# Split weights in half-tile buffers: six of 1024 columns in place of three of 2048

## The chip, the cores and the metric

The kernel runs on one core of one Trainium2 chip. The metric is the device time of one execution in microseconds; the number to predict is the median of the runs of the changed kernel.

## The reference

A trunk of two layers on one sequence of 256 tokens, width 1024, all in float32. Layer 0 mixes tokens by a mixture of three dilated sliding-window attentions, layer 1 by a gated linear attention (GLA); behind each stands a gated ConvFFN of inner width 2816. Each sub-layer is normed, and shifted, scaled and gated by a conditioning vector c.

```python
for i in range(DEPTH):                                   # DEPTH = 2
    mod = jax.nn.silu(c) @ w_ada[i] + b_ada[i]
    sh1, sc1, g1, sh2, sc2, g2 = jnp.split(mod, 6, axis=-1)
    h = rmsnorm(x, norm_mix[i]) * (1.0 + sc1) + sh1
    y = dilated_mixture(h, ...) if i % 2 == 0 else gla_mixer(h, ...)
    x = x + g1 * y
    h = rmsnorm(x, norm_ffn[i]) * (1.0 + sc2) + sh2
    x = x + g2 * conv_ffn(h, w_up[i], conv_w[i], conv_b[i], w_down[i])
return rmsnorm(x, norm_final)

def dilated_mixture(h, w_in, w_out, rel_bias):
    qkv = (h @ w_in).reshape(B, S, 3, 3, 16, 64)         # 3 groups, q k v, 16 heads
    outs, lses = zip(*[dilated_branch(...) for window, dilation in ((128, 1), (512, 4), (2048, 16))])
    o = jnp.sum(jax.nn.softmax(jnp.stack(lses), axis=0)[..., None] * jnp.stack(outs), axis=0)
    return o.reshape(B, S, 1024) @ w_out

def conv_ffn(h, w_up, conv_w, conv_b, w_down):
    u = conv_b + sum(conv_w[j] * shifted(h @ w_up, j) for j in range(3))
    a, b = jnp.split(u, 2, axis=-1)
    return (jax.nn.silu(a) * b) @ w_down
```

## The kernel before

Activations lie transposed, 128 channels of the width by 256 tokens in a tile, so that a width of 1024 is eight slices, kt = 0 to 7. Nearly all matrix products are made by `mm3` (lines 171 to 177) in three matmuls: each operand is split into a high part (rounded to the format fp32r) and a low part (the rest), and high times high (L175), low times high (L176) and high times low (L177) are summed in PSUM. Of the normed activations the parts are `hhi` and `hlo`, made by `normed` (L253): VectorE (DVE) writes `xr` (L257), ScalarE (ACT) `hhi` (L259), DVE `hlo` (L260). Of the weights they are `whi` and `wlo`, made by `split`: SyncE (SP) issues the load into `raw` (L159), ACT casts it to `whi` in two halves (L165), DVE subtracts to get `wlo` in two halves (L169). A tile of raw weights has up to 2048 columns. There are four buffers of `raw`, three of `whi` and three of `wlo`. A buffer is free for the next tile when the last product that reads it is done; so a cast to `whi` waits for matmuls. `parts` picks the columns of one product out of a split tile. Some other tiles share the buffers of `whi` and `wlo`: the conditioning row and the one-hot table of the bias at the start, the squares of x, and the output y at the end.

The order of the work is the scheduler's. The kernel is written down in program order, the tile framework schedules it with a timeline of its own, and pools, waits and `behind(...)` (an instruction isn't issued before the named ones) shape what comes out. Each engine then takes its instructions strictly in the order of the program so made, and each transfer is issued in the order of SP's queue.

The stages, in order of time:

- The start and the first pass. Loads of x, c and small tables, the first norm; then, for each kt, a tile of adaLN weights (`ada_chunk`: DVE makes two dot products at L138, ACT two `mod` columns at L148 and L146), `normed`, and `split` of the tile `w0[kt]` of 15 x 128 columns: six blocks of q and k of head pair 0, three of v, six of q and k of head pair 1. Eight PSUM banks sum the products over kt: `pqk` (q and k of pair 0), `pv`, `pqk1` (q and k of pair 1). The tile of kt = 0 is loaded by two transfers.
- Attention, eight head pairs u: the weights of q and k of a group (`wqk`, 2048 columns), of v (`wv`, 1536 columns in each of two halves), evacuation of q, k, v from PSUM, scores s (L419 in split products, L426 in plain float32), softmax, transposes t (L457), po (L462, L466), all woven with the products of the next pair. Tiles of adaLN weights are read between them.
- `project`: the output projection (`py`), the residual (L322), squares and their sums (`sq` L199, `sqacc` L202), and the next norm (`ms`, L187).
- ConvFFN: 22 tiles of `w_up` of 2048 columns (`pab`), the convolution and the gate, then 32 tiles of `w_down` of 11 x 128 columns (`pd`).
- GLA: products for v (`pv`), log gates, per head k and q (`pqk`), transposes of keys (`kdt` L816, copied by ACT to `kdT` L817), intra-chunk products `a` (L822, masked by DVE to `a_t` L825), states (`kv` L832, `st` L837 and L839), outputs `o` (L855, L858), their squares `osq` (L865), and the gates r (`pr`). `project` and ConvFFN follow, and the last norm.

Products of the plain float32 kind (s of L426, t, po, kdt, a, kv, o, ms) and those of split operands alternate on TensorE (PE; its weight loads are PEld).

Of the kernel before, what the change touches and what calls it, by code (L numbers as in the profile page):

```python
# [57 lines left out]
def trunk(ctx: ExitStack, tc: tile.TileContext, I, out):  # L58
# [3 lines left out]
    const = ctx.enter_context(tc.tile_pool(name="const", bufs=1))  # L62
    state = ctx.enter_context(tc.tile_pool(name="state", bufs=1))
    wraw = ctx.enter_context(tc.tile_pool(name="wraw", bufs=4))
    wspl = ctx.enter_context(tc.tile_pool(name="wspl", bufs=3))
    tmp = ctx.enter_context(tc.tile_pool(name="tmp", bufs=3))
    psum = ctx.enter_context(tc.tile_pool(name="psum", bufs=2, space=PSUM))
    dram = ctx.enter_context(tc.tile_pool(name="dram", bufs=1, space=bass.MemoryType.DRAM))
# [11 lines left out]
            nc.scalar.preload_act_table_set(EXP_LN)  # L80


    c_row = wspl.tile([P, 2048], F32, tag="whi", name="c_row")
    nc.scalar.dma_start(c_row[:1, :D], I["c"])

    x_all = state.tile([P, KT, T], F32, name="x_all")
# [9 lines left out]
    oh = wspl.tile([P, 2048], F32, tag="whi", name="oh")  # L96
    nc.scalar.dma_start(oh[:33, :NROW], I["onehot"])

    def col(at):
# [50 lines left out]
        return last  # L150


    last_load, copied, last_lo = [None], [None], [None]

    def split(src, n, dmas=1, after=((), ()), late=(), low=()):
        raw = wraw.tile([P, 2048], F32, tag="raw", name="raw")
        for i in range(dmas):
            c = slice(n * i // dmas, n * (i + 1) // dmas)
            last_load[0] = nc.sync.dma_start(raw[:, c], src[:, c])  # L159
        hi = wspl.tile([P, 2048], F32R, tag="whi", name="whi")  # L160
        lo = wspl.tile([P, 2048], F32R, tag="wlo", name="wlo")
        for i in range(0, n, n // 2):
            c = slice(i, i + n // 2)
            with behind(*after[i > 0]):
                copied[0] = nc.scalar.copy(hi[:, c], raw[:, c])  # L165
        for i in range(0, n, n // 2):
            c = slice(i, i + n // 2)
            with behind(*(late if i else low)):
                last_lo[0] = nc.vector.tensor_tensor(lo[:, c], raw[:, c], hi[:, c].bitcast(F32), op=ALU.subtract)  # L169
        return hi, lo  # L170

    def mm3(ps, a, b, start, stop):

# [150 lines left out]
            squared[1] = i  # L324

    def parts(w, at, n=P):
        return w[0][:, at : at + n], w[1][:, at : at + n]

# [19 lines left out]
        return b[:, :]  # L348


    sq = wspl.tile([P, 2048], F32, tag="wlo", name="sq").rearrange("p (k t) -> p k t", k=KT)
    with behind(last_c):
        keep_warm(4)
    nc.vector.tensor_tensor(sq[:, 0:4, :], x_all[:, 0:4, :], x_all[:, 0:4, :], op=ALU.mult)
    with behind(silu):
        for i in (4, 6):
            last_sq = nc.scalar.activation(sq[:, i : i + 2, :], x_all[:, i : i + 2, :], AF.Square)
    for n in (0, 4):
        for m in (2, 1):
            last_add = nc.vector.tensor_tensor(sq[:, n : n + m, :], sq[:, n : n + m, :], sq[:, n + m : n + 2 * m, :], op=ALU.add)  # L360
# [4 lines left out]
    r = rstd_of([sq[:, 0, :], sq[:, 4, :]])  # L365

    rows_ps, at = [], 0
    with behind(norm_ops[0]):
# [9 lines left out]
    for kt in range(KT):  # L378
        with behind(*first):
            term = ada_chunk(0, kt, dmas=1 if kt else 2)  # L380
        h.append(normed(0, 0, r, kt))
        if kt:
            w0.append(split(I["w0"][kt], 15 * P))
        else:
            with behind(chain[0][1]):
                w0.append(split(I["w0"][kt], 15 * P, 2, after=((term,), (chain[0][0],))))
            with behind(copied[0]):
                for ps, c in rows_ps:
                    nc.scalar.copy(rows[:, c], ps)
            first = (last_lo[0],)  # L390
        if kt == 1:
            scale_terms(1)
# [116 lines left out]
    for u in range(NPAIR):  # L509
# [10 lines left out]
        if u == 0:  # L520
            b0 = [bank("pqk", tg) for tg in "ssspp"]
            pqk = [b[:, T * i : T * i + T] for b in b0[:3] for i in range(2)]
            pv = b0[3:]
            b1 = [bank("pqk", "t") for _ in range(3)]
            pqk1 = [b[:, T * i : T * i + T] for b in b1 for i in range(2)]
            for kt in range(KT):
                s, e = kt == 0, kt == KT - 1
                for i in range(2 * NG):
                    mm3(pqk[i][:, :T], parts(w0[kt], P * i), h[kt], s and i % 2 == 0, e and i % 2 == 1)
                wv = parts(w0[kt], 6 * P, NG * P)  # L530
                for t in range(2):
                    ht = [y[:, P * t : P * t + P] for y in h[kt]]
                    mm3(pv[t][:, : NG * P], ht, wv, s, e)
                for i in range(2 * NG):
                    mm3(pqk1[i], parts(w0[kt], 9 * P + P * i), h[kt], s and i % 2 == 0, e and i % 2 == 1)
        if u < 2:
            for g in range(NG):
                evacuate(q, k, g, (pqk, pqk1)[u][2 * g], (pqk, pqk1)[u][2 * g + 1])
# [64 lines left out]
    def ffn(l, early):  # L603
# [4 lines left out]
        with tc.tile_pool(name=f"ffn{l}", bufs=2) as pool:  # L608
# [57 lines left out]
            for f2 in range(0, KT, 2):  # L666
                pd = [bank("pd") for _ in range(2)]
                if l == 1:
                    next_ada()
                for half, f in ((0, 0), (0, 1), (1, 0), (1, 1)):  # L670
                    w = split(I["w_down"][l, f2 + f, half], 11 * P)
                    for j in range(11):
                        i = 11 * half + j
                        last_pd[0] = mm3(pd[f][:, :T], parts(w, P * j), (g_hi[i], g_lo[i]), i == 0, i == NFF - 1)
                early = load_early(I["w_qk_b"][0]) if (l, f2) == (0, 6) else None
                for f in range(2):
                    residual(l, 1, f2 + f, pd[f][:, :T])
# [294 lines left out]
    y = wspl.tile([P, 2048], F32, tag="whi", name="y")  # L972
    for half in range(2):
        for t, own in enumerate(halves):
            c = slice(512 * half, 512 * half + 512)
            d = y[:, D * t : D * t + D][:, c]
# [29 lines left out]
def _laid_out(a):  # L1006
# [3 lines left out]
    def vec(v):  # L1010
# [76 lines left out]
```

## Time and profile before

| | us |
|---|---|
| median of three runs | 789.2 (789.19, 789.20, 790.78) |
| profiled execution, its own time | 786.27 |
| span of its instructions | 784.5 |
| PE busy | 769.3 |
| DVE busy | 644.3 |
| ACT busy | 481.8 |

Mean granted clock of TensorE: 0.996. HBM read: 182.59 MB, 234 GB/s over the span.

The profile's times are of one execution, taken by the hardware profiler. PE's busy time is the union of pipelined matmuls whose ends are modelled: a matmul of 256 columns is shown with 0.28 us, and in a dense stretch the next one starts 0.11 us after it. "Idle before" a group is time in which its engine did nothing just ahead of it, with what ended it behind the arrow.

### The profile page before, as it was taken

The page shows a single profiled execution, that of the slowest core. Times are in us where ns is not written, and L with a number is a line of the kernel's source. Part 1 is how long each engine was busy: PE and PEld are TensorE (multiplying, and loading weights), DVE is VectorE, ACT ScalarE, POOL GpSimd, SP SyncE. Part 2 cuts the span into 40 slices and gives each one's busy share as a digit, 9 for nine tenths or more (in the row PEclk, how much of TensorE's full clock was granted, in tenths as well). Part 3 has the DMA queues.
Part 4 walks back from the last instruction along what each step waited for, and adds up shares of the span by engine and source line. Part 5 has one row for each costly group of instructions (what it writes and reads, how often), then busy time and mean ns, then how long its engine had stood idle before and what let it go on. Part 6 is the DMA issues. An engine that isn't in the chain of part 4 may idle for free.

```text
span 784.5 us, 15887 instructions
## 1 busy us (share of the span) xinstructions
PE 769.3 (98%) x6416; PEld 741.2 (94%) x6416; DVE 644.3 (82%) x1160; ACT 481.8 (61%) x940; POOL 14.3 (2%) x40
## 2 busy tenths in 40 slices
PE   8999999999999998999999999999999999999997
PEld 5999999999999997999999999898999999999997
DVE  6998978878789858999998886797567898899762
ACT  5566555545555657876666555665667866667552
POOL 1000000000000010000000000000010000000000
PEclk9999999999999999999999999999999999999999
DMA  9999577585785726777555985966445765655651
GB/s 347 419 325 343 191 288 264 197 322 195 266 292 200 271 102 227 264 262 267 188 177 201 314 324 183 343 229 229 147 137 190 259 203 178 211 177 210 237 184 54
DMA packets 32616, 184.72 MB, mean 235 GB/s; under 512 B 5852, under 2 KB 7388, under 8 KB 16286
## 3 DMA queue, kind: packets, MB, share of 16 engines
q1 hardware_dynamic: 32160, 183.26, 65.3%
q8 instruction: 50, 0.82, 0.4%
q10 hardware_dynamic: 382, 0.45, 0.2%
q14 instruction: 24, 0.20, 0.1%
HBM read 182.59 MB, written 1.10 MB: 234 GB/s over the span
## 4 chain that ended last, share of the span: by engine, by line
PE 91%; DMA 3%; DVE 3%; ACT 2%; issue 1%; SPq 0%; ACTq 0%; DVEq 0%
PE pab L176 10%; PE pab L175 10%; PE pab L177 10%; PE pqk L175 7%; PE pqk L176 6%; PE pqk L177 6%; PE pd L175 5%; PE pd L177 5%; PE pd L176 5%; PE pv L175 3%; PE pv L176 3%; PE pv L177 3%; PE py L175 2%; PE s L419 2%; PE py L176 2%; PE py L177 1%
## 5 line engine op out<-in xcount | busy, mean ns | idle before, releaser
L169 DVE TENSOR_TENSOR wlo<-raw,whi 128x1024 fp32r<-128x1024 f32 (+3 forms) x274 | 291.8, 1095 | 50.7 <-ACT whi L165 47.9
L165 ACT CAST whi<-raw 128x1024 fp32r<-128x1024 f32 (+3 forms) x274 | 245.7, 944 | 131.5 <-PE pab L176 38.3
L176 PE MATMUL pab<-hlo,whi 128*128 128x256 f32 x672 | 184.8, 276 | 0.0
L177 PE MATMUL pab<-hhi,wlo 128*128 128x256 f32 x672 | 184.8, 276 | 0.0
L175 PE MATMUL pab<-hhi,whi 128*128 128x256 f32 x672 | 183.5, 277 | 0.0
L176 PEld LDWEIGHTS pab<-hlo,whi 128*128 128x128 f32 x672 | 126.1, 188 | 0.2
L177 PEld LDWEIGHTS pab<-hhi,wlo 128*128 128x128 f32 x672 | 126.1, 188 | 0.0
L175 PEld LDWEIGHTS pab<-hhi,whi 128*128 128x128 f32 x672 | 125.3, 188 | 0.1
L175 PE MATMUL pqk<-hhi,whi 128*128 128x256 f32 x440 | 120.7, 286 | 3.6 <-ACT hhi L259 3.0
L176 PE MATMUL pqk<-hlo,whi 128*128 128x256 f32 x440 | 122.0, 281 | 0.0
L138 DVE CUSTOM_DVE_ANT_0 ada_raw<-ada_raw,c_bc 128x1024 f32<-128x1024 f32 x96 | 113.4, 1218 | 10.2 <-DMA ada_raw<-in_w_ada 8.8
L177 PE MATMUL pqk<-hhi,wlo 128*128 128x256 f32 x440 | 121.7, 281 | 0.0
L177 PE MATMUL pd<-ghi,wlo 128*128 128x256 f32 x352 | 97.1, 276 | 0.0
L176 PE MATMUL pd<-glo,whi 128*128 128x256 f32 x352 | 97.1, 276 | 0.0
L175 PE MATMUL pd<-ghi,whi 128*128 128x256 f32 x352 | 96.8, 276 | 0.0
L175 PEld LDWEIGHTS pqk<-hhi,whi 128*128 128x128 f32 x440 | 81.7, 190 | 5.1 <-ACT hhi L259 3.5
L177 PEld LDWEIGHTS pqk<-hhi,wlo 128*128 128x128 f32 x440 | 82.6, 188 | 0.9 <-issue 0.7
L176 PEld LDWEIGHTS pqk<-hlo,whi 128*128 128x128 f32 x440 | 82.8, 188 | 0.4
L177 PEld LDWEIGHTS pd<-ghi,wlo 128*128 128x128 f32 x352 | 66.1, 188 | 0.0
L176 PEld LDWEIGHTS pd<-glo,whi 128*128 128x128 f32 x352 | 66.1, 188 | 0.0
L175 PEld LDWEIGHTS pd<-ghi,whi 128*128 128x128 f32 x352 | 65.9, 188 | 0.0
L648 ACT ACTIVATE r<-pab,small 128x256 f32<-128x256 f32 x86 | 46.5, 559 | 19.2 <-DVE r L651 19.2
(215 smaller groups left out, 1304.5 us busy)
## 6 DMA issues: line engine op xcount, KB each, us to landing
ada_raw<-in_w_ada SPq DMA_DIRECT2D x47, 1024.0 KB, 6.8
raw<-in_w_up SPq DMA_DIRECT2D x42, 1024.0 KB, 4.9
raw<-in_w_down SPq DMA_DIRECT2D x32, 704.0 KB, 5.5
raw<-in_wqk SPq DMA_DIRECT2D x18, 1024.0 KB, 7.4
raw<-in_wv SPq DMA_DIRECT2D x14, 768.0 KB, 4.5
raw<-in_w SPq DMA_DIRECT2D x7, 960.0 KB, 6.8
raw<-in_w_out_a SPq DMA_DIRECT2D x4, 1024.0 KB, 7.2
raw<-in_w_v_b SPq DMA_DIRECT2D x4, 1024.0 KB, 6.1
```

What stands on the lines that cost most here:

```text
L138: nc.vector.tensor_tensor_reduce(w, w, c_bc, op0=ALU.mult, op1=ALU.add, scale=1.0, scalar=0.0, accum_out=dot,)
L165: copied[0] = nc.scalar.copy(hi[:, c], raw[:, c])
L169: last_lo[0] = nc.vector.tensor_tensor(lo[:, c], raw[:, c], hi[:, c].bitcast(F32), op=ALU.subtract)
L175: mm(ps, a[0], b[0], start=start, stop=False)
L176: mm(ps, a[0], b[1], start=False, stop=False)
L177: return mm(ps, a[1], b[0], start=False, stop=stop)
L419: mm(s[:, 0:n], q[0][a][:, r].rearrange("p a b -> p (a b)"), k[0][b][:, 0:n], start=(i == 0), stop=(i == 2))
L648: nc.scalar.activation(r, u[:, :T], AF.Identity, scale=cw[2], bias=col(C_CB + 44 * l + f))
```

## The change

The pools of `whi` and `wlo` hold six buffers of 1024 columns each in place of three of 2048. `split` makes two pieces of a tile, each with a `whi` and a `wlo` of its own, cut at a column that no product straddles (in the middle, at 8 x 128 of 15 x 128 for w0, at 6 x 128 of 11 x 128 for w_down); a tile of up to 1024 columns takes one piece. A piece's buffer is free when the products of its own columns are done. So that v's three blocks lie in one piece, the columns of `w0` are reordered: q and k of pair 0, then the first two blocks of pair 1, then v, then the other four. The squares of x and the output y take two tiles each. The bytes loaded, the matmuls and the space taken are the same.

```diff
-    wspl = ctx.enter_context(tc.tile_pool(name="wspl", bufs=3))
+    wspl = ctx.enter_context(tc.tile_pool(name="wspl", bufs=6))
...
-    def split(src, n, dmas=1, after=((), ()), late=(), low=()):
+    def split(src, n, dmas=1, after=((), ()), late=(), low=(), cut=None):
+        cut = cut or (n // 2 if n > 1024 else n)
         raw = wraw.tile([P, 2048], F32, tag="raw", name="raw")
-        for i in range(dmas):
-            c = slice(n * i // dmas, n * (i + 1) // dmas)
+        for c in (slice(0, cut), slice(cut, n)) if dmas > 1 else (slice(0, n),):
             last_load[0] = nc.sync.dma_start(raw[:, c], src[:, c])
-        hi = wspl.tile([P, 2048], F32R, tag="whi", name="whi")
-        lo = wspl.tile([P, 2048], F32R, tag="wlo", name="wlo")
-        for i in range(0, n, n // 2):
-            c = slice(i, i + n // 2)
-            with behind(*after[i > 0]):
-                copied[0] = nc.scalar.copy(hi[:, c], raw[:, c])
-        for i in range(0, n, n // 2):
-            c = slice(i, i + n // 2)
+        pieces = []
+        for c in (slice(0, cut), slice(cut, n)):
+            if c.stop > c.start:
+                hi = wspl.tile([P, 1024], F32R, tag="whi", name="whi")
+                lo = wspl.tile([P, 1024], F32R, tag="wlo", name="wlo")
+                pieces.append((c.start, c.stop, hi, lo, raw[:, c]))
+        ops = [(hi[:, 0 : b - a], lo[:, 0 : b - a], r) for a, b, hi, lo, r in pieces]
+        if n == 1024:
+            ops = [tuple(z[:, c] for z in ops[0]) for c in (slice(0, 512), slice(512, n))]
+        for i, (hi, lo, r) in enumerate(ops):
+            with behind(*after[i]):
+                copied[0] = nc.scalar.copy(hi, r)
+        for i, (hi, lo, r) in enumerate(ops):
             with behind(*(late if i else low)):
-                last_lo[0] = nc.vector.tensor_tensor(lo[:, c], raw[:, c], hi[:, c].bitcast(F32), op=ALU.subtract)
-        return hi, lo
+                last_lo[0] = nc.vector.tensor_tensor(lo, r, hi.bitcast(F32), op=ALU.subtract)
+        return pieces
...
     def parts(w, at, n=P):
-        return w[0][:, at : at + n], w[1][:, at : at + n]
+        for first, end, hi, lo, _ in w:
+            if first <= at and at + n <= end:
+                return hi[:, at - first : at - first + n], lo[:, at - first : at - first + n]
+        assert False
...
-            w0.append(split(I["w0"][kt], 15 * P))
+            w0.append(split(I["w0"][kt], 15 * P, cut=8 * P))
...
-                w0.append(split(I["w0"][kt], 15 * P, 2, after=((term,), (chain[0][0],))))
+                w0.append(split(I["w0"][kt], 15 * P, 2, cut=8 * P, after=((term,), (chain[0][0],))))
...
-                wv = parts(w0[kt], 6 * P, NG * P)
+                wv = parts(w0[kt], 8 * P, NG * P)
...
-                    mm3(pqk1[i], parts(w0[kt], 9 * P + P * i), h[kt], s and i % 2 == 0, e and i % 2 == 1)
+                    mm3(pqk1[i], parts(w0[kt], P * (i + (6 if i < 2 else 9))), h[kt], s and i % 2 == 0, e and i % 2 == 1)
...
-                    w = split(I["w_down"][l, f2 + f, half], 11 * P)
+                    w = split(I["w_down"][l, f2 + f, half], 11 * P, cut=6 * P)
...
             qk[:, :, :, :, 0].reshape(KT, P, 6 * P),
+            qk[:, :, 0, :, 1].reshape(KT, P, 2 * P),
             w[:, :, :, 2, 0].reshape(KT, P, 3 * P),
-            qk[:, :, :, :, 1].reshape(KT, P, 6 * P),
+            qk[:, :, 1:, :, 1].reshape(KT, P, 4 * P),
```

In the changed kernel the lines of `split` are L160 (load), L172 (cast) and L175 (subtraction); those of `mm3` are L181 to L183, and of `normed` L263, L265 and L266.

More of the change, by code (lines that the diff above doesn't have):

```diff
@@ L80, in exp_ln_after @@
             nc.scalar.preload_act_table_set(EXP_LN)
-    c_row = wspl.tile([P, 2048], F32, tag="whi", name="c_row")
+    c_row = wspl.tile([P, 1024], F32, tag="whi", name="c_row")
     nc.scalar.dma_start(c_row[:1, :D], I["c"])
@@ L95, in trunk @@
     nc.vector.memset(tab[32:33, :], 1.0)
-    oh = wspl.tile([P, 2048], F32, tag="whi", name="oh")
+    oh = wspl.tile([P, 1024], F32, tag="whi", name="oh")
     nc.scalar.dma_start(oh[:33, :NROW], I["onehot"])
@@ L348, in load_bias @@
         return b[:, :]
-    sq = wspl.tile([P, 2048], F32, tag="wlo", name="sq").rearrange("p (k t) -> p k t", k=KT)
+    sq = [wspl.tile([P, 1024], F32, tag="wlo", name="sq").rearrange("p (k t) -> p k t", k=4) for _ in range(2)]
     with behind(last_c):
         keep_warm(4)
-    nc.vector.tensor_tensor(sq[:, 0:4, :], x_all[:, 0:4, :], x_all[:, 0:4, :], op=ALU.mult)
+    nc.vector.tensor_tensor(sq[0], x_all[:, 0:4, :], x_all[:, 0:4, :], op=ALU.mult)
     with behind(silu):
         for i in (4, 6):
-            last_sq = nc.scalar.activation(sq[:, i : i + 2, :], x_all[:, i : i + 2, :], AF.Square)
+            last_sq = nc.scalar.activation(sq[1][:, i - 4 : i - 2, :], x_all[:, i : i + 2, :], AF.Square)
     for n in (0, 4):
         for m in (2, 1):
-            last_add = nc.vector.tensor_tensor(sq[:, n : n + m, :], sq[:, n : n + m, :], sq[:, n + m : n + 2 * m, :], op=ALU.add)
+            s = sq[n // 4]
+            last_add = nc.vector.tensor_tensor(s[:, 0:m, :], s[:, 0:m, :], s[:, m : 2 * m, :], op=ALU.add)
         if n == 0:
@@ L364, in trunk @@
     exp_ln_after(last_sq)
-    r = rstd_of([sq[:, 0, :], sq[:, 4, :]])
+    r = rstd_of([s[:, 0, :] for s in sq])
     rows_ps, at = [], 0
@@ L971, in trunk @@
     nc.scalar.activation(r, ln, AF.Exp, scale=-0.5)
-    y = wspl.tile([P, 2048], F32, tag="whi", name="y")
+    y = [wspl.tile([P, D], F32, tag="whi", name="y") for _ in halves]
     for half in range(2):
@@ L975, in trunk @@
             c = slice(512 * half, 512 * half + 512)
-            d = y[:, D * t : D * t + D][:, c]
+            d = y[t][:, c]
             if t:
```

## The prediction

> **What bounds the kernel now.** I read the page first (busy time by engine), then who TensorE waited for, then the start of the kernel instruction by instruction.
>
> ```profile
> span 784.5 us, 15887 instructions
> PE 769.3 (98%) x6416; PEld 741.2 (94%) x6416; DVE 644.3 (82%) x1160; ACT 481.8 (61%) x940; POOL 14.3 (2%) x40
> ...
> L165 ACT CAST whi<-raw 128x1024 fp32r<-128x1024 f32 (+3 forms) x274 | 245.7, 944 | 131.5 <-PE pab L176 38.3
> ```
>
> TensorE is busy for 769.3 of 784.5 us, so it bounds the kernel and 15.2 us is all that can be won by taking idle time away. The casts that fill the whi buffers do wait for matmuls (38.3 us of the 131.5 idle before L165 is ended by pab matmuls, that is by a buffer coming free). This is the wait that the change goes for. But it is idle time of ACT. What matters is who TensorE itself waits for:
>
> ```profile
> PE pqk L175 <- ACT hhi L259: 3.0, 2, 2.4
> PE ms L187 <- DVE sqacc L202: 2.5, 1, 2.5
> PE cb L123 <- DMA c_row<-in_c: 2.3, 1, 2.3
> PE pqk L175 <- ACT v L504: 0.6, 1, 0.6
> PE o L855 <- DVE a_t L825: 0.6, 1, 0.6
> PE pr L177 <- DVE wlo L169: 0.5, 1, 0.5
> ...
> PE pv L175 <- DVE k L483: 0.2, 1, 0.2
> ```
>
> Columns: total us, times, longest. Split weights appear once, for 0.5 us (pr, in the GLA stage). Earlier release of their buffers can directly win that 0.5 us and little else. So the change acts mainly through the order in which the scheduler now issues instructions: TensorE, ACT and DVE each take theirs in the program's order, and that order was made anew. I read both programs' orders (no time is in them) and priced the places where they differ.
>
> **The start: one moved step, on the path.** The largest wait, 2.4 us for hhi, is that of the second slice (kt=1) of the first pass. Before, on ACT, SP and TensorE:
>
> ```profile
> 16.91 1.90 ACT L165 CAST whi<-raw 128x960 fp32r<-128x960 f32 x2 [2.38 <-DMA raw<-in_w]
> 18.71 0.29 ACT L148 ACTIVATE mod<-dot,small 128x1 f32<-128x1 f32 x1
> 18.91 0.37 ACT L146 ACTIVATE mod<-dot,one_b,small 128x1 f32<-128x1 f32 x1
> 20.61 0.51 ACT L259 ACTIVATE hhi<-xr,mod 128x256 fp32r<-128x256 f32 x1 [1.32 <-DVE xr L257]
> 21.74 1.89 ACT L165 CAST whi<-raw 128x960 fp32r<-128x960 f32 x2 [0.62 <-DMA raw<-in_w]
> 23.53 0.29 ACT L148 ACTIVATE mod<-dot,small 128x1 f32<-128x1 f32 x1
> 23.73 0.37 ACT L146 ACTIVATE mod<-dot,one_b,small 128x1 f32<-128x1 f32 x1
> ```
> ```profile
> 15.54 0.33 SPq L159 DMA_DIRECT2D raw<-in_w  x1
> ```
> ```profile
> 18.44 0.28 PE L177 MATMUL pqk<-hhi,wlo 128*128 128x256 f32 x1
> 21.17 1.01 PE L175 MATMUL pqk<-hhi,whi 128*128 128x256 f32 x3 [2.45 <-ACT hhi L259]
> ...
> 27.80 0.52 PE L175 MATMUL pqk<-hhi,whi 128*128 128x256 f32 x3
> ```
>
> The casts of slice 1 run at 16.91, hhi of slice 1 at 20.61, and TensorE starts slice 1 at 21.17, 0.56 us after hhi starts. The casts of slice 2 come after that, at 21.74, when their load lands (the row's releaser is the DMA; it was issued at 15.54). In the changed program ACT's order is another:
>
> ```
> L172 TensorCopy whi<-raw 128x1024      slice 1
> L172 TensorCopy whi<-raw 128x896
> L148 Activation mod   L146 Activation mod
> L172 TensorCopy whi<-raw 128x1024      slice 2, now ahead
> L172 TensorCopy whi<-raw 128x896
> L148 Activation mod
> L265 Activation hhi<-xr,mod 128x256    slice 1
> ```
>
> Both casts of slice 2 now stand ahead of hhi of slice 1, and the first of them still waits for its load. SP's order up to there is the same and the load waits for the same raw buffer, so it lands at 21.74 again. The casts hold ACT until 23.53 (as before: the mod behind them started at 23.53), that mod until 23.73, so hhi starts at 23.73 instead of 20.61: 3.12 us later, and TensorE's slice 1 starts at 23.73 + 0.56 = 24.29. DVE has to be ready by then:
>
> ```profile
> 17.95 2.23 DVE L169 TENSOR_TENSOR wlo<-raw,whi 128x960 fp32r<-128x960 f32 x2
> 20.09 0.48 DVE L257 SCALAR_TENSOR_TENSOR xr<-x_all,mod,rstd 128x256 f32<-128x256 f32 x1
> 20.49 1.22 DVE L138 CUSTOM_DVE_ANT_0 ada_raw<-ada_raw,c_bc 128x1024 f32<-128x1024 f32 x1
> ```
>
> On DVE one adaLN dot (1.15 us to the next start) now stands ahead of xr of slice 1: 20.09 + 1.15 + 0.40 = 21.64, before 21.74, so ACT decides. Then come the second dot (to 22.79), both wlo of slice 2 (2.14, to 24.93) and hlo of slice 1 (to 25.3). TensorE needs hlo after ten products of hhi alone, which took 21.17 to 23.90 before; 24.29 + 2.73 = 27.0, so hlo is no new wait. The first cast is also 1024 wide instead of 960, and hhi of slice 0 stands behind it: 64/960 of 0.95 us, +0.06 us.
>
> Does TensorE catch up? It does only where it waited for something that does not come later with it.
>
> ```profile
> 18.60:21.10 2.50, 0.12 (x2) 0.00 (x0) 2.50 (x4) 1.18 (x4) 0.00 (x0) 0.91 1.00 411
> 21.10:24.00 2.90, 2.83 (x11) 2.83 (x12) 2.90 (x6) 2.28 (x5) 0.00 (x0) 0.50 1.02 423
> 24.00:27.00 3.00, 3.00 (x27) 3.00 (x27) 3.00 (x6) 1.00 (x3) 0.00 (x0) 0.99 1.04 424
> ...
> 21.10:57.00 35.90, 35.83 (x278) 35.84 (x279) 35.08 (x54) 21.12 (x37) 0.00 (x0) 0.96 0.97 374
> ```
>
> Columns: length, busy PE, PEld, DVE, ACT, POOL, granted clock, DMA share, GB/s. From 21.1 to 57 us TensorE is busy for 35.83 of 35.90, so it has no slack to give. Of the later waits only those for v, a_t, k and wlo (1.9 us together) could absorb anything, and their releasers are fed by TensorE too. I let all 3.1 us pass; bounds +1.2 (all 1.9 absorbed) and +3.6 (a load 0.5 us later).
>
> The window rows show one more price. After the wait the clock is 0.50 for 2.9 us and full again by 24. Slice 1 took 21.17 to 27.80, 6.63 us; later slices take 5.2 (next rows), so this costs 1.4 us already now and does so once more after a longer wait. [...]
>
> ```profile
> 33.17 0.53 PE pqk L175 x4
> 36.15 0.46 PE pqk L177 x3
> 38.38 0.53 PE pqk L175 x4
> ```
>
> **GLA.** Before, the ten products o of head 1 covered ACT's copy kdT of head 3. Now the transposes come behind these products and the state products follow at once, and ACT runs osq ahead of kdT.
>
> ```profile
> 536.17 0.60 ACT L865 ACTIVATE osq<-o 128x512 f32<-128x512 f32 x1 [0.33 <-PE o L858]
> 536.66 0.37 ACT L817 COPY kdT<-kdt 128x256 f32<-128x256 f32 x1
> ...
> 537.22 0.48 PE L832 MATMUL kv<-v,kdT 64*128 64x256 f32 x1
> ```
>
> From osq's start to the kv product are 1.05 us, with about 0.25 us of transposes beside it: +0.8. In return 32 of head 0's gate products now stand between a of head 3 and the next o, so the waits for a_t (0.6) and wlo (0.5) go: −1.1. Next late is the state st2 of head 3, which DVE now makes behind six wlo of 1.1 us each: my estimate by adding up its queue is 0.7 us late. Net +0.4, between −1.1 (nothing new is late) and +1.5.
>
> **Changes between kinds of products.** Each change from plain float32 products (s, t, po, o) back to the split ones costs; here after po:
>
> ```profile
> 102.05 0.45 PE L175 MATMUL pv<-whi,hhi 128*128 128x384 f32 x1
> 102.33 0.34 PE L176 MATMUL pv<-wlo,hhi 128*128 128x384 f32 x1
> 102.51 0.34 PE L177 MATMUL pv<-whi,hlo 128*128 128x384 f32 x1
> ```
>
> Starts are 0.28 apart instead of 0.18: 0.1 us. The new order has 85 such returns instead of 90: −0.5 us, between 0 and −1.3 (if the product ahead loses as much again, and somewhat more).
>
> **What costs nothing.**
>
> ```profile
> 302.00:390.00 88.00, 88.00 (x775) 87.91 (x775) 84.73 (x149) 65.36 (x121) 0.00 (x0) 1.00 0.71 244
> ```
>
> Bytes, loads, matmuls (6078 in both) and column sums are the same; only w_glr's split loses one cast and one subtraction. Halves of 768 and 640 instead of 704 and 704 columns mean the same ACT and DVE time, under a TensorE that is busy for 88.00 of 88.00 us in the first FFN. The columns of w0 are only renamed. The wait of 2.5 us for sqacc stays: both programs have the two casts of w_up ahead of the last squares on ACT; the new one has six more py products and one more early product behind kt=6 (+0.9 of cover) but reaches those casts later; I take 0, ±0.5.
>
> **Sum.** 3.12 + 0.06 + 0.4 − 0.5 = +3.1 us. The profiled execution took 786.27 us (span 784.5), which gives 789.4 for a profiled one; the median of the runs shown is 789.2, 2.9 above it, and I add the difference there: 792.3 us.
>
> **Rivals.**
> (a) The finer release lets ACT and DVE run ahead, and the waits for v, a_t, wlo and k all go (1.9), with 1.3 from fewer changes of kind and none of GLA's new waits: 3.18 − 3.2, about 789.2, no change. For it: 38.3 us of casts waiting for matmuls. Against: TensorE hardly waited for casts. It decides if TensorE's waits after 60 us sum to under 3 us.
> (b) The forecast's own place turns out the other way, faster: the load of slice 2 lands before ACT gets to it, by 18.9 us, so that the casts are over by 20.7 and hhi is as early as before; with the −0.5 and half of (a), 787.5. Against: it is issued at 15.54 and DMA is at 1.00 and 411 GB/s then, so 6.2 us can hardly become 3.4.
> (c) The 2.5 us wait for sqacc grows and the clock falls there:
>
> ```profile
> 295.00:298.00 3.00, 0.50 (x3) 0.20 (x2) 2.58 (x5) 1.06 (x4) 0.00 (x0) 1.00 0.62 251
> ```
>
> It stayed at 1.00 before; the wait at the start lost it. Price as at the start, 1.4 us, plus up to 0.5 of longer wait and GLA's upper end (1.1 more): 795.3. [...]
> (d) The change does nothing for the time because the order of ACT matters less than it seems: 789.2.
>
> **How the numbers follow.** The forecast gets 0.64, (a) 0.14, (b) 0.05, (c) 0.13, (d) 0.04. A measurement of this kernel can tell about 0.2% (1.6 us) from no change. Slower: the forecast and (c), 0.77, and a little of (a), 0.79. Within 0.2%: most of (a), and (d), 0.15. Faster: (b) and a little of (a), 0.06. The range runs from 789.8 (forecast less 1.9 absorbed and less 0.6 at GLA) to 795.8 (just over (c)); it leaves out most of (a), (b) and (d).
>
> **What would show it.** Right: hhi of slice 1 starts near 23.7 us behind two casts that a DMA ends, TensorE idles about 5.6 us before it, and the clock is 0.5 for some 3 us behind. TensorE's waits after 60 us sum to about as much as before. Wrong: slice 1 starts near 21 us, or it starts late and the total is yet not later; then a wait that I counted as staying has gone.

## The result, and the profile after

| | before | after |
|---|---|---|
| median of six runs each, us | 789.2 (786.35 to 790.78) | 792.92 (791.81 to 793.93) |
| ratio after to before | | 1.0052, 95% interval 1.0034 to 1.0070 |
| profiled execution, its own time | 786.27 | 792.91 |

The change makes the kernel slower by 0.34 to 0.70%, and the forecast was 792.3. (The ratio is taken over all runs; the medians alone lie 0.47% apart.) The two profiled executions lie 6.6 us apart, more than the medians (3.7), since the profiled one of before was 2.9 us quicker than its median.

The page of the changed kernel, span and busy time by engine, and one group (casts to whi):

```profile
span 791.1 us, 15977 instructions
...
PE 772.1 (98%) x6416; PEld 744.7 (94%) x6416; DVE 647.5 (82%) x1159; ACT 486.9 (62%) x939; POOL 12.2 (2%) x40
...
L172 ACT CAST whi<-raw 128x1024 fp32r<-128x1024 f32 (+3 forms) x273 | 252.5, 949 | 158.3 <-PE pab L182 56.0
```

The casts wait for matmuls more than before (56.0 instead of 38.3 us): probably ACT gets to the next buffer sooner with finer ones and then waits there, which no run separates. TensorE has the same 6416 products. It is busy with them for 2.8 us longer (772.1 against 769.3) and idle for 19.0 us, 3.8 more than before. Who it waited for in the changed kernel (total us, times, longest):

```profile
PE pqk L181 <- ACT hhi L265: 5.8, 2, 5.4
PE kdt L826 <- DVE k_d L818: 2.5, 1, 2.5
PE ms L193 <- DVE sqacc L208: 2.3, 1, 2.3
...
PE kv L842 <- ACT kdT L827: 0.7, 1, 0.7
```

The wait for hhi grew from 3.0 to 5.8 us, waits for k_d and for kdT are new, that for sqacc is about as it was (2.3 against 2.5). Those for v, a_t, wlo and k are gone. The start on ACT and on TensorE, and the windows behind it (length, busy PE, PEld, DVE, ACT, POOL, granted clock, DMA share, GB/s):

```profile
16.74 1.90 ACT L172 CAST whi<-raw 128x1024 fp32r<-128x1024 f32 x2 [2.23 <-DMA raw<-in_w]
18.55 0.29 ACT L148 ACTIVATE mod<-dot,small 128x1 f32<-128x1 f32 x1
18.74 0.37 ACT L146 ACTIVATE mod<-dot,one_b,small 128x1 f32<-128x1 f32 x1
21.58 1.88 ACT L172 CAST whi<-raw 128x1024 fp32r<-128x1024 f32 x2 [2.47 <-DMA raw<-in_w]
23.37 0.29 ACT L148 ACTIVATE mod<-dot,small 128x1 f32<-128x1 f32 x1
23.57 0.49 ACT L265 ACTIVATE hhi<-xr,mod 128x256 fp32r<-128x256 f32 x1
```
```profile
18.39 0.28 PE L183 MATMUL pqk<-hhi,wlo 128*128 128x256 f32 x1
24.12 1.01 PE L181 MATMUL pqk<-hhi,whi 128*128 128x256 f32 x3 [5.45 <-ACT hhi L265]
```
```profile
21.10:24.00 2.90, 0.00 (x0) 0.00 (x0) 2.90 (x7) 2.42 (x5) 0.00 (x0) 0.51 1.00 414
24.00:27.00 3.00, 2.88 (x11) 2.88 (x12) 3.00 (x6) 1.38 (x4) 0.00 (x0) 0.50 1.02 422
27.00:30.00 3.00, 3.00 (x23) 3.00 (x22) 3.00 (x5) 1.83 (x4) 0.00 (x0) 0.83 1.02 417
```

ACT stands idle from 19.1 to 21.58 for the load of slice 2, with hhi of slice 1 behind its casts, and TensorE for 5.45 us with it. Then the clock is half until 28 us. The second place is GLA's head 0. Before, on DVE and TensorE:

```profile
513.51 1.75 DVE L750 TENSOR_TENSOR_SCAN cs<-keep,sp 128x768 f32<-128x768 f32 x1
515.17 1.20 DVE L169 TENSOR_TENSOR wlo<-raw,whi 128x1024 fp32r<-128x1024 f32 x1
516.29 0.42 DVE L809 SCALAR_TENSOR_TENSOR q_t<-early_q,e_q 128x256 f32<-128x256 f32 x1
516.63 0.42 DVE L808 TENSOR_TENSOR k_d<-pqk,e_d 128x256 f32<-128x256 f32 x1
...
518.16 1.22 DVE L138 CUSTOM_DVE_ANT_0 ada_raw<-ada_raw,c_bc 128x1024 f32<-128x1024 f32 x1
```
```profile
518.84 0.38 PE L816 MATMUL kdt<-ident,k_d 128*128 128x128 f32 x2
```

After, on TensorE and on DVE:

```profile
522.62 0.28 PE L183 MATMUL pqk<-hhi,wlo 128*128 128x256 f32 x1
525.43 0.44 PE L826 MATMUL kdt<-ident,k_d 128*128 128x128 f32 x2 [2.53 <-DVE k_d L818]
```
```profile
519.54 0.42 DVE L819 SCALAR_TENSOR_TENSOR q_t<-early_q,e_q 128x256 f32<-128x256 f32 x1
519.88 1.22 DVE L138 CUSTOM_DVE_ANT_0 ada_raw<-ada_raw,c_bc 128x1024 f32<-128x1024 f32 x1
...
521.02 1.22 DVE L138 CUSTOM_DVE_ANT_0 ada_raw<-ada_raw,c_bc 128x1024 f32<-128x1024 f32 x1
...
522.17 1.75 DVE L760 TENSOR_TENSOR_SCAN cs<-keep,sp 128x768 f32<-128x768 f32 x1
523.84 1.20 DVE L175 TENSOR_TENSOR wlo<-raw,whi 128x1024 fp32r<-128x1024 f32 x1
524.95 0.42 DVE L818 TENSOR_TENSOR k_d<-pqk,e_d 128x256 f32<-128x256 f32 x1
```
```profile
527.00:530.00 3.00, 3.00 (x16) 2.78 (x17) 3.00 (x5) 1.59 (x4) 0.00 (x0) 0.54 0.95 347
```

Before, k_d followed q_t at once, and the first kdt waited for nothing. Now k_d comes behind two adaLN dots, the scan over 768 columns and a wlo, 5.1 us in all (519.88 to 524.95). TensorE runs out of products at 522.9 and waits 2.5 us, and the clock is half behind this wait too (0.54 in the last row).

Each stage's length follows from the start times of its first product in the timeline (us; stages: start from the first pqk to the first s; attention and project up to the first ms of sqacc; from there to the first pab; first FFN up to the first z; GLA from z to the first kdt, and from there to the second pab; the rest):

| profiled execution | start | attention | ms to pab | FFN | z to kdt | kdt to pab | rest |
|---|---|---|---|---|---|---|---|
| before | 51.85 | 233.03 | 3.85 | 200.72 | 16.47 | 80.08 | 185.54 |
| after | 54.10 | 232.94 | 5.54 | 201.26 | 18.65 | 80.11 | 185.56 |
| before, second profile | 51.56 | 232.54 | 5.01 | 201.03 | 16.47 | 79.98 | 185.55 |
| after, second profile | 54.82 | 232.94 | 3.85 | 200.95 | 18.94 | 80.06 | 186.02 |

What differs in both pairs is the start (2.2 and 3.3 us) and GLA up to kdt (2.2 and 2.5). The column ms to pab changes with the execution and not with the kernel.

### The profile page after: what moved, and what is told of

Same layout as the page of the kernel before. It is cut to its first block, busy times and chain, and to the rows that moved or that the text cites. A ratio compares the mean times of both kernels' runs of the same rounds, so it can differ in the third digit from the quotient of the medians.

```text
span 791.1 us, 15977 instructions
## 1 busy us (share of the span) xinstructions
PE 772.1 (98%) x6416; PEld 744.7 (94%) x6416; DVE 647.5 (82%) x1159; ACT 486.9 (62%) x939; POOL 12.2 (2%) x40
## 4 chain that ended last, share of the span: by engine, by line
PE 90%; DVE 4%; ACT 3%; DMA 2%; issue 1%; ACTq 0%; DVEq 0%
PE pab L181 10%; PE pab L183 10%; PE pab L182 10%; PE pqk L181 7%; PE pqk L182 6%; PE pqk L183 6%; PE pd L183 5%; PE pd L182 5%; PE pd L181 5%; PE pv L181 3%; PE pv L183 2%; PE pv L182 2%; PE s L429 2%; PE py L181 2%; PE py L182 2%; PE py L183 2%
## 5 line engine op out<-in xcount | busy, mean ns | idle before, releaser
L172 ACT CAST whi<-raw 128x1024 fp32r<-128x1024 f32 (+3 forms) x273 | 252.5, 949 | 158.3 <-PE pab L182 56.0
L175 DVE TENSOR_TENSOR wlo<-raw,whi 128x1024 fp32r<-128x1024 f32 (+3 forms) x273 | 295.4, 1099 | 62.1 <-ACT whi L172 60.3
L183 PE MATMUL pab<-hhi,wlo 128*128 128x256 f32 x672 | 185.0, 276 | 0.0
L181 PE MATMUL pab<-hhi,whi 128*128 128x256 f32 x672 | 183.7, 277 | 0.0
L181 PE MATMUL pqk<-hhi,whi 128*128 128x256 f32 x440 | 122.6, 287 | 5.8 <-ACT hhi L265 5.8
L183 PEld LDWEIGHTS pab<-hhi,wlo 128*128 128x128 f32 x672 | 126.2, 188 | 0.0
L181 PEld LDWEIGHTS pab<-hhi,whi 128*128 128x128 f32 x672 | 125.3, 188 | 0.1
L182 PE MATMUL pqk<-hlo,whi 128*128 128x256 f32 x440 | 123.6, 284 | 0.0
L183 PE MATMUL pqk<-hhi,wlo 128*128 128x256 f32 x440 | 123.0, 283 | 0.0
L183 PE MATMUL pd<-ghi,wlo 128*128 128x256 f32 x352 | 97.2, 276 | 0.0
L181 PE MATMUL pd<-ghi,whi 128*128 128x256 f32 x352 | 97.2, 276 | 0.0
L181 PEld LDWEIGHTS pqk<-hhi,whi 128*128 128x128 f32 x440 | 83.1, 192 | 7.1 <-ACT hhi L265 6.2
L183 PEld LDWEIGHTS pqk<-hhi,wlo 128*128 128x128 f32 x440 | 83.6, 191 | 0.5 <-issue 0.3
L181 PEld LDWEIGHTS pd<-ghi,whi 128*128 128x128 f32 x352 | 66.1, 188 | 0.0
L183 PEld LDWEIGHTS pd<-ghi,wlo 128*128 128x128 f32 x352 | 66.1, 188 | 0.0
L182 PE MATMUL pv<-wlo,hhi 128*128 128x384 f32 (+1 forms) x144 | 50.3, 349 | 0.0
```

The costliest lines, as they stand in the source:

```text
L172: copied[0] = nc.scalar.copy(hi, r)
L175: last_lo[0] = nc.vector.tensor_tensor(lo, r, hi.bitcast(F32), op=ALU.subtract)
L181: mm(ps, a[0], b[0], start=start, stop=False)
L182: mm(ps, a[0], b[1], start=False, stop=False)
L183: return mm(ps, a[1], b[0], start=False, stop=stop)
```

## The experiments

**How an order is held.** A scheduler makes the order, and any edit reshuffles all of it. So most kernels here are traced twice. The first trace records the order of all 8,284 instructions; then a few are moved in that list, and in the second trace each instruction is chained to its predecessor in the list, by an edge for the order alone that adds no wait.

```python
for a, b in zip(order, order[1:]):
    tc.add_manual_dep(program[b], program[a].name,
                      mybir.DependencyInfo(mybir.DependencyClass.NoSync, mybir.DependencyReason.DATA), reason="replay")
```

So a diff below can be one instruction in one queue, with everything else where it was; in the traces of runs 2, 3, 6 and 7 each engine's order differs from the changed kernel's in the moved instructions alone. No run holds the changed kernel's own order with nothing moved or added, so what holding an order costs or wins by itself is not measured. Runs 1 to 4, 5 to 8, 9 and 10, and 11 and 12 shared a chip each and the runs of the kernel before on it (medians 787.98, 788.80, 788.02 and 788.68 us).

**1. The old order on the new buffers.** My theory was that the order makes the difference; the rival, that buffers do.

```diff
 # buffers, cuts and columns of the change
-order = as the scheduler makes it
+order = that of the kernel before
```

> The change with the instruction order of the kernel before: six half-tile buffers and the reordered columns as in the change, but every engine issues its instructions in the order that the kernel before had (two tiles excepted, the first of w_out_a and of w_r_b, whose second half can no longer be cast ahead of the first and comes right behind it). My theory (the change acts through the new order; released half tiles win at most 0.5 us directly): 788.5 to 789.5 us, hhi of slice 1 starts near 20.6 us, TensorE starts slice 1 near 21.2 us, GLA's first kdt waits for nothing; against the kernel before 0 to -0.5 us. Rival 1 (the finer release is worth microseconds by itself and the new order only hides that): 787 or less. Rival 2 (the cut itself costs, by the uneven pieces or the second buffer's waits): 791 or more.

Measured: 789.56 us, 1.0023 of before (1.0013 to 1.0032). A little over half of the loss goes with the old order (0.23% is left of 0.52). But finer buffers win nothing. My theory had 0 to -0.5 us against the kernel before, and the run is 1.6 us over it, short of the 791 of rival 2. In the profiles attention is 0.7 us longer than in the second one of before (233.21 against 232.54), and GLA from kdt on 0.8 (80.83 against 79.98). One new wait there is at a place that this order had to change, where a second half of w_r_b is cast later, and DVE and oacc with it:

```profile
PE ms L193 <- DVE oacc L877: 0.6, 1, 0.6
```

**2. hhi of slice 1 alone put back.**

```diff
 ACT:
+L265 hhi<-xr,mod          slice 1
 L172 whi<-raw  L172 whi<-raw   slice 2
-L265 hhi<-xr,mod          slice 1
 DVE: xr of slice 1 ahead of the first dot of slice 2
```

> The changed kernel with its own order, and two instructions moved back to where the kernel before had them: on ACT hhi of slice 1 ahead of the two casts of slice 2, on DVE xr of slice 1 ahead of the first dot of slice 2. My theory: hhi starts at 20.6 instead of 23.57 us, TensorE starts slice 1 at 21.2 instead of 24.12, nothing else moves: 792.9 - 3.0 = 789.9 us. Rival 1 (the start's delay is absorbed later, the order of ACT matters less than it seems): 792 to 793. Rival 2 (an earlier slice 1 runs into another wait, for hlo or for the load of slice 2, and keeps half): 791.4.

Measured: 792.84 us, 1.0059 (1.0039 to 1.0079), as slow as the changed kernel. TensorE in this run:

```profile
PE pqk L181 <- ACT hhi L265: 3.5, 2, 2.3
PE s L429 <- DVE m L447: 3.1, 2, 1.7
...
PE pqk L182 <- DVE hlo L266: 2.6, 1, 2.6
```

Slice 1 started 2.4 us sooner and then waited 2.6 us for hlo, which the new DVE order has behind both wlo of slice 2. So hhi was only the first of two late steps: rival 2 has the mechanism, rival 1 the time. This profile is of the longest of the six executions, 798.84 us, 6 us over the median. In its attention two waits of s for m were new, 3.1 us. Run 3 has them too (1.8 us) and run 10 has one (0.8), runs 5 to 7 have none, and what brings them stays open.

**3. k_d and k_t of head 0 put back.**

```diff
 DVE:
 L819 q_t
+L818 k_d  L820 k_t
 L138 dot  L138 dot  L760 cs  L175 wlo
-L818 k_d  L820 k_t
```

> The changed kernel with its own order, and two DVE instructions of GLA's head 0 moved: k_d and k_t right behind q_t, ahead of two adaLN dots, the scan over 768 columns and a wlo, behind which the changed order puts them. Theory (the first kdt waits 2.5 us for k_d because of these four, and the clock is half for some 3 us behind that wait, 17 products at 0.21 instead of 0.11 us): the wait goes and the clock stays at 1.0, 792.9 - 2.5 - 1.7 = 788.7 us. Rival 1 (the wait goes, but the scan and e_q behind it make the next step late and take half back): 790.8. Rival 2 (the clock falls there anyway): 790.4.

Measured: 791.20 us, 1.0042 (1.0026 to 1.0059). The theory's 788.7 is missed by 2.5 us, and the gain in the time is not clear of noise: the changed kernel has 1.0052 and, in run 5, 1.0057, with overlapping intervals. In the trace GLA from z to the first py falls from 72.81 to 70.46 us (before: 70.59). TensorE's waits in GLA:

```profile
PE kv L842 <- ACT kdT L827: 1.7, 2, 0.9
PE kdt L826 <- DVE k_d L818: 1.0, 1, 1.0
```

The 2.5 us wait is gone; a k_d of a later head waits 1.0, and ACT's kdT 1.0 more. So the first rival's mechanism is there too, and 2.3 us are won in GLA in this trace. Its attention is 2.7 us longer than the changed kernel's (235.60 against 232.94), with the waits of s for m, and hides that.

**4. The kernel before once more.**

> The kernel before, unchanged, for a second profile of it and the clock of several executions. The profiled execution of before took 786.27 us, 2.9 less than the median of the runs. Theory: in the usual execution the clock falls to half for about 3 us at the wait for sqacc near 295 us, which it did not do in the profiled one; then a typical execution shows a mean clock of 0.994 or less beside 0.996, and 788 to 791 us, and runs with 0.996 are near 786. Rival (the spread is in the transfers, and the clock is 0.996 in all): times between 786 and 791 at one and the same clock.

Measured: 788.65 us, 1.0001 (0.9989 to 1.0014), profiled 786.82. My theory falls, and the rival's mark is there: at one mean clock of 0.996 there are executions of 786.21 and of 789.39 us. The profiled one did have the half clock behind the wait for sqacc:

```profile
297.00:299.40 2.40, 2.40 (x6) 1.72 (x7) 1.47 (x2) 1.06 (x3) 0.00 (x0) 0.50 0.05 20
```

It is quick all the same. What makes an execution of this kernel 3 us longer than another stays open.

**5. The changed kernel once more.**

> The changed kernel, unchanged, beside the others of this group. In the two runs made from its order so far attention took 235.6 and 238.6 us from the first s to the sums of squares, with new waits of s for DVE's m behind casts that a load ended late; in the first profile of the changed kernel it took 232.9, and in the old order 232.5 to 233.2 on the same chip. Theory 1 (the new order has loads in attention that land just in time, so it pays where transfers are some per cent slower): 793 to 796 us here and attention 235 us or more. Theory 2 (those waits came from the moved instructions): 792 to 793 and attention 233.

Measured: 793.65 us, 1.0057 (1.0038 to 1.0077), attention 232.94 us. Neither theory is confirmed: the median is that of theory 1, attention that of theory 2. But attention was profiled in one of the two quick executions (792.32 us; both show a mean clock of 0.994). The other four, of 793.4 us and more, show 0.990 or 0.991, so part of their time goes with the clock; their attention isn't known.

**6. The start mended: hhi, xr and hlo.**

```diff
 as in run 2, and on DVE:
+L266 hlo<-xr,mod,hhi      slice 1
 L175 wlo  L175 wlo        slice 2
-L266 hlo<-xr,mod,hhi      slice 1
```

> The changed kernel with its own order and three instructions of slice 1 moved: hhi on ACT ahead of the casts of slice 2, xr on DVE ahead of the first dot of slice 2, and, new, hlo on DVE ahead of the two wlo of slice 2. With the first two alone TensorE started slice 1 2.5 us earlier and then waited 2.6 us for hlo. Theory (the start's 2.5 us lie in three moved steps, hhi and hlo one behind the other): from the first pqk to the first s 51.8 us instead of 54.1, and 2.3 us less than the changed kernel in this group. Rival (DVE is the bound of the first pass, so that what slice 1 wins is lost by slice 2): 53.5 us, and 0.5 less.

Measured: 789.54 us, 1.0015 (1.0001 to 1.0030), 4.1 less than run 5. The start is 51.15 us instead of 54.82 (its first pqk came 0.75 us later than in run 5, so that the first s is 2.9 us sooner). TensorE's waits there:

```profile
PE pqk L181 <- ACT hhi L265: 1.5, 2, 0.8
PE pqk L182 <- DVE hlo L266: 1.4, 2, 0.9
```

The theory had 2.3 us, the rival 0.5. In this profile the clock is 1.00 from 21 to 30 us, so the half clock behind the long wait is gone with it; it was half earlier, during slice 0, whose products start 0.21 us apart from 15.57 to 17.49 and 0.11 to 0.12 from 17.86 on, so that TensorE came later to the wait for hhi, and this is shorter than the 2.3 us of run 7. Three instructions in other places of two queues are most of what the change costs (4.1 of 4.85 us in this group).

**7. Start and keys mended.**

```diff
 the moves of run 6 and of run 3
```

> The changed kernel with the start mended (hhi, xr and hlo of slice 1 moved) and GLA's k_d and k_t of head 0 moved ahead of the dots and the scan. Theory (start and GLA are the two places where the new order costs, and they add): 2.3 for the start and 1 to 2.5 for GLA, 3.3 to 4.8 us less than the changed kernel in this group, so about the time of the kernel before. Rival (a third place, attention, holds the rest): the same gain, but still 2 us or more over the kernel before.

Measured: 788.90 us, 0.9995 (0.9981 to 1.0010): the changed kernel with five instructions moved takes the time of the kernel before, 4.75 us less than run 5, as the theory had it. Start 51.20, GLA from z to py 70.58 us, as before the change. Over run 6 the medians win only 0.6 us, and the intervals overlap, while the trace shows 2.3 in GLA; between these the size of GLA's share stays uncertain.

**8. The kernel before, mended.** The waits around hhi and sqacc are in the kernel before too, only shorter.

```diff
 each slice k of the first pass, from 1
 ACT:  whi  +mod +mod  whi  -mod -mod  hhi
 DVE:  wlo  +xr  wlo  +hlo  -xr  dot dot (slice k+1)  -hlo
 project: three products "early" ahead of ms instead of behind it
```

> The kernel before with whole buffers and its own order but for two places. First pass, each slice from 1 on: ACT does the mod columns between the two casts, DVE does xr between the two wlo and hlo right behind them, ahead of the next slice's dots. Project: three of the early products go into the wait for sqacc, ahead of ms. Theory (what these 5 us around hhi, hlo and sqacc cost is order, not buffers): TensorE starts slice 1 at about 20.0 instead of 21.2 us and slice 2 at 25.4 instead of 27.5, and the clock stays up at sqacc in more executions: 2.5 to 3.5 us less than the kernel before, 785. Rival (DVE, busy for 35.1 of 35.9 us there, gives no more than 1 us): 787 to 788.

Measured: 785.62 us, 0.9958 (0.9942 to 0.9974): faster than both kernels, by 3.2 us against the one before, as the theory had it. Six of its seven executions show a mean clock of 1.000. The windows of the start and of sqacc, and TensorE's waits:

```profile
18.60:21.10 2.50, 1.33 (x9) 1.22 (x9) 2.50 (x5) 1.03 (x2) 0.00 (x0) 1.00 1.02 423
21.10:24.00 2.90, 2.90 (x26) 2.90 (x25) 2.90 (x5) 2.12 (x4) 0.00 (x0) 1.00 1.01 418
...
294.00:299.00 5.00, 3.63 (x15) 2.25 (x13) 3.84 (x7) 2.11 (x6) 0.00 (x0) 1.00 0.38 120
```
```profile
PE pqk L175 <- ACT hhi L259: 1.4, 2, 1.2
PE ms L187 <- DVE sqacc L202: 1.2, 1, 1.2
```

TensorE starts slice 1 at 19.88 and slice 2 at 25.27 us, the start is 50.06, and behind both short waits the clock is 1.00.

**9. The mended order on half-tile buffers.**

```diff
 buffers of the change, order of run 8
 w_out_a and w_r_b, first tile: both halves cast at the place of the first one cast before
```

> The order of the mended kernel before (first pass and early products as in the run before this one, 785.6 us with whole buffers, 0.9958 of the kernel before), but with six half-tile buffers and the reordered columns of the change. The first tiles of w_out_a and w_r_b, whose halves the old order casts second half first, are cast together at the earlier place. It answers what the change's buffers are worth when order and waits are the same. Theory (nothing: TensorE waits for no cast in that order): 785 to 786 us. Rival 1 (the half-tile buffers cost about 1.5 us by themselves, as the run with the plain old order gave 789.6 against 788.0): 787. Rival 2 (they win once the larger waits are gone): 784.5 or less.

Measured: 786.68 us, 0.9986 (0.9972 to 1.0000), with a wide spread (784.5 to 790.5). The median is over the theory's 785 to 786 and near rival 1's 787; run 8, of the same order with whole buffers, is from another chip. Runs 11 and 12 set the two side by side.

**10. The wait at the start filled with idle products.**

```diff
 # changed kernel, its own order; behind the last product of slice 0
+for _ in range(18):
+    mm(pv[0][:, 384:512], ones_d, ones_d, start=False, stop=False)
```

> The changed kernel with its own order and 18 plain float32 products of 128 columns (results unused, into columns of a PSUM bank that nothing reads) between the last product of slice 0 and the wait for hhi of slice 1, about 4.1 us of the 5.5 us wait. The wait stays, hhi comes at the same time. Theory (behind the wait the clock is half for 3 us, and that is a price of the idle time, not of the wait): the granted clock stays at 1.0 from 24 to 27 us, slice 1 takes 5.3 instead of 6.6 us, and the kernel 1.3 us less than the changed one, 0.2% of the 0.57% that it is over the kernel before. Rival 1 (slice 1 then waits for hlo, which comes at 25.3 us, and slice 2 for its hhi, so nothing is won): the changed kernel's time. Rival 2 (dummies delay the first product of slice 1): slower by up to 0.5.

Measured: 791.96 us, 1.0039 (1.0024 to 1.0053), against 1.0057 for the changed kernel in run 5; the intervals overlap, so the gain is not clear of noise in the time. The windows:

```profile
21.10:24.00 2.90, 2.40 (x22) 2.21 (x20) 2.90 (x6) 2.28 (x4) 0.00 (x0) 1.00 1.00 393
24.00:27.00 3.00, 2.65 (x18) 2.45 (x19) 3.00 (x5) 0.99 (x3) 0.00 (x0) 1.00 1.01 380
```

Slice 1 began at 24.25 us, as late as in the changed kernel, and the clock stayed at 1.00. From there to the first s it took 41.5 us instead of 42.9 and 43.7. So in these profiles the half clock is a price of TensorE's idleness, of 1.4 us or more, on top of the wait.

**11 and 12. Whole and half-tile buffers side by side, in the mended order.**

> The mended kernel before (whole buffers) once more, now beside its twin with half-tile buffers on the same chip. Theory (buffers are worth nothing, order is all): 785.6 us, and the twin within 0.5 us of it. Rival (half-tile buffers cost in this order): 785.6, and the twin 1 to 2 us over it.

> The same order on six half-tile buffers, beside the run with whole ones. In the single run of it so far the median was 786.7, between 784.5 and 790.5, and its profile showed waits for k (1.4 us) and for hhi (0.6 and 0.9) that the one with whole buffers lacks. Theory (buffers are worth nothing): within 0.5 us of the run with whole buffers. Rival (they cost, by casts and subtractions that now run at other times): 1 to 2 us more, with a wait for k at the end of attention again.

Measured: whole 785.18 us, 0.9957 (0.9943 to 0.9972); halves 786.28, 0.9971 (0.9955 to 0.9986). The theory's 0.5 us is missed. Halves are slower by 1.1 us in the medians and by 1.5 in the means of twelve runs each (standard error 0.45, worked out from their times), as the rival had it, with the wait for k that it named. DVE near the end of attention, first whole, then halves:

```profile
260.01 1.23 DVE L169 TENSOR_TENSOR wlo<-raw,whi 128x1024 fp32r<-128x1024 f32 x1 [2.31 <-ACT whi L165]
261.15 0.42 DVE L483 COPY k<-pqk 128x256 f32<-128x256 f32 x1
```
```profile
260.03 2.36 DVE L175 TENSOR_TENSOR wlo<-raw,whi 128x1024 fp32r<-128x1024 f32 x2 [2.50 <-ACT whi L172]
262.31 0.42 DVE L493 COPY k<-pqk 128x256 f32<-128x256 f32 x1
```

With halves two wlo stand ahead of k instead of one, because this run casts that tile's halves one right behind the other, and TensorE waits 1.9 us for k instead of 0.4. Attention is 235.09 us instead of 233.60. This one place, 1.5 us, is as much as the whole difference; GLA from kdt on is 0.7 us shorter in return (79.23 against 79.97). That the buffers would be worth nothing with this place mended is argued from the trace and not shown by a run. No run shows a gain from them.

## Why the prediction was right, point by point

**What bounds the kernel, and what finer buffers win directly: right.** At most 0.5 us was given to them. Runs 1 and 12 have them with an order taken from the whole buffers, and are 1.6 and 1.1 us slower than those.

**The start: right in place and size, incomplete in its cause.** hhi was forecast at 23.73 and TensorE's slice 1 at 24.29; they came at 23.57 and 24.12, behind two casts that a DMA ended. The clock was half behind the wait for 3.9 us (24.12 to 28.00), and in the second profile for 5.6 (24.03 to 29.66), instead of "some 3". If half of that is lost, as the 1.4 of 2.9 us before, it costs 1.9 and 2.8 us (an estimate); the working left the 1.4 unchanged. Slice 1 began 2.95 us later in the first pair of profiles and 2.9 in the second; the first s came 2.3 and 3.3 us later. So TensorE made up some of it in the first pair, and none in the second. What the working missed is how close the next step was. It showed that hlo would be no new wait in the changed kernel, which is true, and left it there. Put hhi back, and hlo is late by itself (run 2); only both together bring the time back (with xr moved too; run 6, 4.1 us).

**The clock: right at the start, wrong elsewhere.** It was 0.50 when the wait of 5.45 us for hhi ended, as forecast, and before when that of 2.45 us did. It fell behind waits of 2.3 to 2.4 us elsewhere too (2.4 at sqacc in run 4, 2.28 there in the changed kernel), and behind one of 2.50 it did not (sqacc in the first profile of before). Rival (c) put its price on sqacc in the changed kernel: 1.7 us there in its first profile and none in its second, though the wait had not grown.

**GLA: the step that failed.** The forecast was +0.4 us, bounds -1.1 and +1.5. Measured from z to the second pab are +2.2 us in the first pair of profiles (98.76 against 96.55) and 2.55 in the second (99.00 against 96.45), outside the bounds. The parts that were named came true: kdT of head 3 waits 0.7, a_t and wlo no longer. What was overlooked is head 0. I followed the order from head 1 on, and did not add up DVE's queue ahead of the first k_d: two dots, a scan and a wlo, 5.1 us, with TensorE out of products. The mis-sized term is this one, 2.5 us of wait in the first profile and 2.8 in the second. The half clock behind it (0.54 in the 3 us window) is not to be told apart in the sum: from kdt to the second pab both kernels take 80.0 to 80.1 us.

**Changes between kinds of products: not confirmed.** -0.5 was forecast for attention, where nearly all of them are. The order does have fewer such returns there (68 instead of 74 in attention, counted in the traces), but attention is 0.1 shorter in one pair of profiles and 0.4 longer in the other, although the waits for v and k (0.8 us together) went.

**FFN at nothing: right within half a us.** The first FFN is 0.5 us longer in one pair and 0.1 shorter in the other, the rest behind the second pab the same in one and 0.5 longer in the other.

**From the profile to the median: two errors against each other.** I worked out +3.1 us on the profiled execution of before and added the 2.9 us by which its median lay above it. Between the profiles the difference is 6.6: the start, GLA and, in these executions, 1.7 at sqacc and 0.5 in the first FFN; between the second profiles it is 5.5. So the sum was too small by 2.4 to 3.5 us, GLA's term alone by about 2. The 2.9 us made up for it, since the changed kernel's profiled execution lay at its median (792.91 and 792.92). What makes the usual execution of before longer than its profiled ones was not found. That the forecast lay 0.6 us from the result is luck in good part; its direction, its first place and that place's size are not.

**Rivals.** (a) has its mechanism: the waits for v, a_t, wlo and k went. It did not decide, since k_d came instead: TensorE's waits after 60 us add up to 5.9 us in the changed kernel and 4.8 before, where (a) needed under 3. (b) failed as argued: the load of slice 2 landed at 21.6. (d) is refuted by run 6.

## What to carry to other kernels

Where a scheduler makes the order, a change to buffers is above all a new order: read the new queues instruction by instruction where the trace of before has its waits, add up each engine's queue ahead of every step that TensorE needs, and do so also where TensorE waits for nothing yet. When a step is found late, ask at once which one is late behind it. To learn what a change is worth by itself, hold the order and change one thing; an order held in this way can then be made better, here by 0.42% against the kernel before (run 8, 0.9958), by moving the small instructions of the first pass ahead of long ones and three products into the wait for sqacc.

## What the hardware showed that was not expected

TensorE's clock fell to 0.50 behind waits well under 3 us: 2.45 us for hhi at the start of the kernel before, 2.4 and 2.28 for sqacc (run 4, and the first profile of the changed kernel), and 1.45 for k in the profile of run 9, a wait that ended at 262.98. Run 9, from the fall on and behind it:

```profile
263.74:267.15 3.41, 3.41 (x13) 3.41 (x12) 1.79 (x5) 3.01 (x8) 0.00 (x0) 0.50 0.87 327
267.20:270.00 2.80, 2.80 (x26) 2.34 (x26) 1.79 (x4) 2.52 (x3) 0.00 (x0) 1.00 0.37 133
```

It stayed at 1.00 behind a wait of 2.3 us in another execution of the same program (sqacc in the changed kernel in run 5, 3.85 us from ms to pab instead of 5.54), behind 1.85 us for k in run 12 (0.999 over the whole execution) and behind 1.2 us in run 8. So the length of the wait alone doesn't tell, and what does was not shown. But for the last microseconds, the half clock lasted from 20.65 to 24.06 us in the first profile of before (3.41 us), and in that of the changed kernel from 21.17 to 28.00 (6.83, around the end of the wait of 5.45), from 301.07 to 304.48 and from 526.35 to 529.76 (3.41 each). The changes of the clock in this last trace lie 6.83, 273.07, 3.41, 221.87 and 3.41 us apart, which is 2, 80, 1, 65 and 1 times 3.413.

In run 9 the executions with a mean clock of 0.999 or 1.000 took 784.5 to 786.5 us and those with 0.995 to 0.997 785.75 to 790.5, so part of the spread goes with the clock. And with 18 idle products from 19.32 to 23.50 us, ahead of the first product of slice 1 at 24.25, it stayed at 1.00 (run 10).
